# One hybrid diffusion layer on one core: value rows copied whole, transposes and first scores tied in the program order, value stores held back, and one table set for log and exp

## The chip, the core and the metric

The kernel runs on one core of one Trainium2 chip. The core has a matrix engine (TensorE, PE in the profile; its weight loads are PEld), a vector engine (VectorE, DVE), a scalar engine for functions and copies (ScalarE, ACT), a general engine (GpSimd, POOL) and a queue that only issues transfers (SyncE, SP). Each engine runs its own instructions strictly in a fixed order, and waits on semaphores where it needs the work of another. The metric is the time of one execution on the device in microseconds (us), as the median of several runs.

## What is computed

One layer of a diffusion backbone over 1024 latent tokens and 256 context tokens, D = 1024, in float32:

```python
px = modulate(rms_norm(x, norm1_w[i]), sh1, sc1) @ w_in[i]
pc = modulate(rms_norm(ctx, norm1_w[i]), csh1, csc1) @ w_in[i]
...
dn_x, _, _ = gated_deltanet(px[..., :DN_IN], ..., s_ctx_f, s_ctx_b)
...
na_x = neighborhood_attention(qx, kx, vx, kc, vc, na_rpb[i], rows)
x = x + g1 * (jnp.concatenate([dn_x, na_x], axis=-1) @ w_out[i])
x = x + g2 * swiglu(modulate(rms_norm(x, norm2_w[i]), sh2, sc2), w_ffn_in[i], w_ffn_out[i])
```

`gated_deltanet` (group A, 4 heads of 128) runs a short convolution and SiLU over q, k and v, builds a triangular system for each chunk, and scans the chunks forward and backward; its output is gated by SiLU(z). `neighborhood_attention` (group B, 8 heads of 64) normalises q and k, and for each query takes one softmax over a window of the 16 x 64 grid and all context keys. All norms are of the form x * rsqrt(mean(x*x) + eps).

## The kernel before

Each float32 operand of a large product is split into a high and a low half, and each product is made of three matmuls (hi*hi, lo*hi, hi*lo): `hh`, `hl` are the halves of the normed input, `whi`, `wlo` those of weights. Casts to the high half are on ACT (L198, L584), the subtractions for the low half on POOL (L199, L585).

**Stages.** The norm and the modulation come first (to about 40 us), then the input projection as a list of jobs (to about 580), then attention and scan together (to 806), the output projection (to 906) and the feed-forward part (to the end).

**The jobs** stand in the list `jobs`: Blocks k0 to k3 and z1, nk0 to nk2, nv0, nk3, q0 to q3, nq0 to nq3, v0, nv1, v1 to v3 and last z0. A Block is one 128-wide column block of the projection: its matmuls go k-step by k-step (L404; a k-step is one of 8 slices of D, six matmuls of 512 columns or a few more), then `evac` copies PSUM out (for a convolution block on ACT, L452, into `cr`; then VectorE makes the five taps, L456 and L460, into `cacc`), `silu` follows on ACT (L467), `norm` for the attention's q and k (nq, nk) takes Ln and Exp on ACT (L492, L494, L496) and then a scale on VectorE, and `finish` makes transposes and stores. For v heads `finish` transposes `cacc` (L526), scales into `vt` (L530) and stores it to `v_d` from ACT's queue (L534). A Wide job (nv: the attention's values, z: the gate) keeps token tiles stationary and takes 256 columns of weights `zw` in two halves of 128, both of which each of its matmuls (L592) reads. Its `prefetch` loads the halves one after the other through one single buffer `wraw` (L583), casts on ACT (L584) and subtracts on POOL (L585). nv tiles are stored to `nv_d`; after each nv job 64 copies in memory (L1104) lay out that half's values by query column block in `vw_d`, and attention loads windows from it (L277).

**Beside the jobs** run two generators, stepped once for each k-step: `block_inverses` (decay tables; inverts all 32 x 32 diagonal blocks of the chunk systems, with a chain on VectorE over the tile `N`, L880 to L885, and then transposes N on PE, L892) and `preps` (for each chunk and direction the rest of the triangular inverse: decay rows `rg` from POOL, L952; their products on PE, L964; Exp on ACT, L968; a product with the key matrix, L984; copies back on ACT, L987; three substitution steps, L995 to L998). A `yield` in them decides how far apart in the jobs their pieces are written; within that, the build orders the instructions of each engine by its own estimate of when they can run, unless an instruction is kept in program order.

**Queues.** SP issues nearly all transfers in one fixed order, and each waits at its head for what it needs. ACT's function tables are loaded by an instruction of their own (ACT_TABLE_LOAD) wherever the next function is not in the set last loaded; the build places these. One column of buffers (`kx`, 3 of them) is shared by `vt`, the gate tile `zg` and others.

**Attention and scan.** `pair` makes the scores of two heads (L302), the bias and softmax (L304 to L308), transposes (L313, L316) and the product with the values (L323). Its first steps are taken between the tiles of z0 (`next(fill)`); the scan (L1212 and on) is mixed in afterwards, and loads v, k, y and others through L1160.

Of the kernel before, what the change touches and what calls it, by code (L numbers as in the profile page):

```python
# [26 lines left out]
NCH = T // 128  # L27
# [61 lines left out]
def hybrid(ctx, tc, a, dbg):  # L89
# [59 lines left out]
    vw_d = dram.tile([128, 4, 4, 4, 128], F32, name="vw_d", tag="vw_d")  # L149
# [23 lines left out]
    act.activation(sc2, c2, AF.Silu)  # L173
    bg = Background()
# [78 lines left out]
    def attention(nw):  # L253
# [21 lines left out]
        def values(hp, half, cb):  # L275
            vw = nw.tile([128, 3, 128], F32, name="vw", tag="vw", bufs=3)
            sp.dma_start(vw, vw_d[:, hp, cb, half:half + 3])  # L277
            return vw

        def context(hp):  # L280
            vc = nw.tile([128, 2, 128], F32, name="vc", tag="vc")
            sp.dma_start(vc, nv_d[0:CT, hp * 128:hp * 128 + 128].rearrange("(c p) d -> p c d", p=128))
            return vc

        def pair(heads, bts, vw, vc, half, cb, out):
# [4 lines left out]
            for u, (head, w0, bt) in enumerate(zip(heads, WIN, bts)):  # L290
                qs, kh, kl = head
                q = qs[:, (half * 4 + cb) * 128:(half * 4 + cb + 1) * 128]
                kv = [kx[:, CT:].rearrange("p (r c) -> p r c", c=64)[:, r0:r0 + 12, BLKS[cb]:BLKS[cb] + 32]
                      for kx in (kh, kl)]
                parts = [(CTX[w0].start, CTX[w0].stop, (kh[:, 0:CT], kl[:, 0:CT]))]
                if w0:
                    parts += [(256, 512, [x[:, 0:8] for x in kv]), (512, 640, [x[:, 8:12] for x in kv])]
                else:
                    parts += [(0, 384, kv)]
                for n0, n1, ks in parts:  # L300
                    for i in range(2):
                        pe.matmul(sc[:, u * 640 + n0:u * 640 + n1], q, ks[i], start=i == 0, stop=i == 1)  # L302
                m = mx[:, u]
                dve.tensor_tensor_reduce(bt, sc[:, u * 640:u * 640 + 640], bt, -1.0, 3.0e38, OP.add, OP.min,  # L304
                                         m[:, 0:1])
# [68 lines left out]
    with ExitStack() as bs:  # L374
# [32 lines left out]
        class Block:  # L407
# [111 lines left out]
            def finish(self):  # L519
                kind, acc, i = self.kind, self.acc, self.i  # L520
                if kind in "kv":
# [12 lines left out]
                    (act if kind == "v" else sp).dma_start(dst[:, i * 128:(i + 1) * 128].rearrange("(c p) d -> p c d", p=128), vt)  # L534
# [5 lines left out]
                if kind in "kq":  # L540
# [20 lines left out]
                    sp.dma_start(dst[:, :, i], kk[:, c0:])  # L561

        class Wide:
# [32 lines left out]
            def tiles(self):  # L596
# [18 lines left out]
                for t in range(2, NCH):  # L615
# [18 lines left out]
                    act.activation(zt[:, :256], p[:, :256], AF.Silu)  # L634
# [132 lines left out]
        def decay_tables(gp):  # L767
# [4 lines left out]
            act.activation(nA, adt[:, 0:8], AF.Exp)  # L772
# [47 lines left out]
        def block_inverses():  # L820
            with ExitStack() as gs:
# [64 lines left out]
                for _ in range(4):  # L886
                    yield
                U = WK.rearrange("p d u i -> p (d u) i")
                for i0 in range(0, 32, 4):
                    p = bank()  # L890
                    for i in range(4):
                        pe.transpose(p[:, i * P:(i + 1) * P], N[:P, :, :, i0 + i].rearrange("p b r -> p (b r)"),  # L892
                                     ident[:P, :P])
# [16 lines left out]
        done = set()  # L910

        def preps():

            first_half.close()
            with ExitStack() as gs:
# [28 lines left out]
                def prep(i, got):  # L944
# [13 lines left out]
                    if i == 0:  # L958
                        yield 1
                    es = []  # L960
                    for d, c, kk, xc, at in got:
                        p = bank("pr")
                        for j in range(2):
                            pe.matmul(p, mr[:, d], fl(rgs[2 * d + j]), start=j == 0, stop=False)  # L964
# [38 lines left out]
                stores, tick = [], [0]  # L1003
# [45 lines left out]
        for n in range(2, len(jobs) + 2):  # L1049
# [47 lines left out]
            if isinstance(j, Wide) and j.kind == "nv":  # L1097
                hv = slice(2 * j.half, 2 * j.half + 2)
                vlat = nv_d[CT:].rearrange("(r c) d -> r c d", c=64)
                for cb in range(4):  # L1100
                    for ch in range(4):
                        for r in range(4):
                            rows = vlat[4 * ch + r, BLKS[cb]:BLKS[cb] + 32].rearrange("c (h d) -> c h d", d=128)
                            sp.dma_start(vw_d[r * 32:r * 32 + 32, hv, cb, ch], rows[:, hv])  # L1104
            if nrm:
                nrm.norm()
            if isinstance(j, Block):
                j.silu()

# [330 lines left out]
    def normed(t):  # L1440

        s, p = HV[t], bank()
        pe.matmul(p, ones, acc[:, s], start=True, stop=True)  # L1443
        act.activation(rs[:, s], p, AF.Ln, bias=b_eps, scale=1.0 / D)
# [328 lines left out]
```

## Time and profile before

| | |
|---|---|
| Median of 3 runs | 1543.63 us |
| Lowest and highest run | 1539.69 and 1545.23 us |
| The profiled execution | 1541.49 us |
| Its span, first to last instruction | 1539.4 us |
| Mean granted clock of TensorE | 0.988 |
| ACT table loads | 39, of 1.28 us each |

The span is what the profile resolves; the 2.1 us around it are not in it. Rows of a timeline give the start, the duration, the engine, the line, the operation and the tiles; in brackets the idle time of that engine just before and what ended it. `x3` at the end of a row stands for several instructions in one stretch. Rows of a view by stretches give busy time for each engine, the clock that TensorE was granted (1.00 is full, 0.50 half) and the mean busy share of the 16 DMA engines.

### The profile page before, as it was taken

To read this page: it belongs to the slowest core of one execution; us is meant where nothing else is said; L and a number is where in the kernel's file an instruction comes from. 1 tells how busy PE (TensorE), PEld (TensorE's weight loads), DVE (VectorE), ACT (ScalarE), POOL (GpSimd) and SP (SyncE) were. 2 spreads that over 40 slices of the span, in tenths; PEclk is the share of its full clock that TensorE was granted. 3 is DMA by queue.
4 is the path that set the end of the run, shared out by engine and by line. 5 is a ranking of instruction groups with operands and counts; after the bars stand their busy time and mean duration, and the time that the engine had idled before them with its cause. 6 is when DMAs were issued, how large, how long until landed. Compare 5 with 4: busy or idle time off the path is not lost. (4 is left out here: it accounts for less than half of the span.)

```text
span 1539.4 us, 24029 instructions
## 1 busy us (share of the span) xinstructions
PE 1474.1 (96%) x8702; PEld 1231.0 (80%) x8702; DVE 993.6 (65%) x1712; ACT 728.2 (47%) x1405; POOL 234.8 (15%) x286
## 2 busy tenths in 40 slices
PE   6999998899899898999999999999999999999999
PEld 3788797777688787788888878888888888888887
DVE  4774587974464354677977379855555566599652
ACT  5442552646764236666873176333333334354440
POOL 1054500634554100111210000000000000000000
PEclk9999999999999999999999999999999999999999
DMA  9274232687655557898638503533333334798742
GB/s 387 68 212 139 60 86 79 202 239 246 182 172 170 147 142 247 278 292 253 209 90 282 183 34 109 186 106 106 107 105 103 104 102 148 248 376 275 247 143 82
DMA packets 205142, 267.36 MB, mean 174 GB/s; under 512 B 17760, under 2 KB 115552, under 8 KB 204000
## 3 DMA queue, kind: packets, MB, share of 16 engines
q1 hardware_dynamic: 194320, 258.45, 52.4%
q10 hardware_dynamic: 10704, 7.38, 1.5%
q8 instruction: 68, 1.11, 0.3%
q14 instruction: 50, 0.41, 0.1%
HBM read 201.02 MB, written 68.94 MB: 175 GB/s over the span
## 5 line engine op out<-in xcount | busy, mean ns | idle before, releaser
L404 PE MATMUL blk<-hh,whi 128*128 128x512 f32 (+1 forms) x410 | 123.0, 394 | 6.8 <-ACT cr L452 5.3
L1410 ACT CAST uhi<-ws 128x512 fp32r<-128x512 f32 x91 | 54.0, 621 | 146.0 <-PE ps L1349 96.1
L1410 ACT CAST uhi<-wq 128x512 fp32r<-128x512 f32 x101 | 61.0, 622 | 130.9 <-issue 84.6
L404 PE MATMUL blk<-hl,whi 128*128 128x512 f32 (+1 forms) x410 | 115.4, 375 | 0.3 <-DVE hl L704 0.3
L404 PE MATMUL blk<-hh,wlo 128*128 128x512 f32 (+1 forms) x410 | 114.6, 375 | 0.6 <-POOL wlo L199 0.6
L592 PE MATMUL blk<-zw,hh 128*128 128x256 f32 (+1 forms) x576 | 113.5, 291 | 1.1 <-ACT cr L452 1.0
L1411 DVE TENSOR_TENSOR ulo<-wq,uhi 128x512 fp32r<-128x512 f32 x101 | 67.5, 687 | 58.4 <-ACT uhi L1410 32.4
L1349 PE MATMUL ps<-hT,uhi 128*128 128x512 f32 x336 | 103.6, 390 | 0.0
L1349 PE MATMUL ps<-lT,uhi 128*128 128x512 f32 x336 | 103.5, 389 | 0.0
L1349 PE MATMUL ps<-hT,ulo 128*128 128x512 f32 x336 | 103.4, 389 | 0.0
L592 PEld LDWEIGHTS blk<-zw,hh 128*128 128x128 f32 x576 | 91.7, 191 | 4.0 <-ACT cr L452 1.5
L1349 PE MATMUL ps<-hB,uhi 128*128 128x512 f32 x288 | 89.2, 391 | 0.6 <-ACT hB L1524 0.6
L1349 PE MATMUL ps<-lB,uhi 128*128 128x512 f32 x288 | 88.8, 389 | 0.4 <-DVE lB L1525 0.4
L1349 PE MATMUL ps<-hB,ulo 128*128 128x512 f32 x288 | 88.6, 389 | 0.0
L404 PEld LDWEIGHTS blk<-hh,whi 128*128 128x128 f32 x410 | 69.0, 194 | 21.9 <-ACT cr L452 6.1
L404 PEld LDWEIGHTS blk<-hl,whi 128*128 128x128 f32 x410 | 72.5, 192 | 14.9 <-DVE hl L704 0.8
L404 PEld LDWEIGHTS blk<-hh,wlo 128*128 128x128 f32 x410 | 72.5, 192 | 14.9 <-POOL wlo L199 0.9
L592 PE MATMUL blk<-zw,hl 128*128 128x256 f32 (+1 forms) x288 | 82.4, 286 | 0.0
L199 POOL TENSOR_TENSOR wlo<-wraw,whi 128x1024 fp32r<-128x1024 f32 x18 | 46.6, 2586 | 194.1 <-ACT whi L198 193.9
L1349 PEld LDWEIGHTS ps<-lT,uhi 128*128 128x128 f32 x336 | 63.1, 188 | 13.2
L1349 PEld LDWEIGHTS ps<-hT,ulo 128*128 128x128 f32 x336 | 63.1, 188 | 13.2
L1349 PEld LDWEIGHTS ps<-hT,uhi 128*128 128x128 f32 x336 | 62.9, 188 | 12.9
(362 smaller groups left out, 3526.1 us busy)
## 6 DMA issues: line engine op xcount, KB each, us to landing
wq<-w_fo SPq DMA_DIRECT2D x99, 256.0 KB, 4.1
wq<-w_gu SPq DMA_DIRECT2D x88, 256.0 KB, 2.9
wad<-wa SPq DMA_DIRECT2D x64, 256.0 KB, 4.2
bt<-rpb SPq DMA_DIRECT2D x64, 192.0 KB, 3.7
t_d<-g SPq DMA_DIRECT2D x22, 512.0 KB, 3.7
fr<-t_d SPq DMA_DIRECT2D x44, 256.0 KB, 5.2
f_d<-g SPq DMA_DIRECT2D x33, 256.0 KB, 2.1
fr<-f_d SPq DMA_DIRECT2D x33, 256.0 KB, 4.2
```

Source lines behind the costliest of these rows:

```text
L199: lo_engine.tensor_tensor(o, r, h.bitcast(F32), OP.subtract)
L404: pe.matmul(o, ww[:, k], xx[k][:, s], start=k == 0 and j == 0, stop=k == KT - 1 and j == 2)
L592: pe.matmul(p[:, :c1 - c0], x[k][:, s], ww[:, k, c0:c1], start=k == 0 and j == 0, stop=k == KT - 1 and j == 2)
L1349: pe.matmul(o, w[wi][:, k], x[xi][:, k], start=first and k == 0 and j == 0, stop=k == n - 1 and j == 2, skip_group_check=True)
L1410: act.copy(hi, self.raw[key])
L1411: dve.tensor_tensor(lo, self.raw[key], hi.bitcast(F32), OP.subtract)
```

## The change

1. **Values in full rows.** `vw_d` is written once, after nv1, by 16 copies of 32 x 4 x 512 values (L1127) instead of 64 copies of 32 x 2 x 128 after each nv job. The load for a head pair takes its 128 columns out of the longer rows.
2. **Stores of v.** v0's store goes out on SP at once; those of v1 to v3 are put in a list and issued on SP by `release()` (L931) after the attention's step between z0's tiles, in program order.
3. **Ties.** The first of each four transposes of N, the first prep's L964 products (now L989) and the first score matmul keep their place in the program; the waiting yields before the transposes are 6 and not 4, and the first prep waits 10 yields there and not 1 (`LATE`).
4. **Tables.** The set with both log and exp is loaded explicitly in four places: behind the first SiLU, at the first Exp of the decay tables (issued behind z1's last gate tile), ahead of the third prep's Exp, and at the feed-forward's norm. The built program has 21 table loads and not 39.

```diff
-    vw_d = dram.tile([128, 4, 4, 4, 128], F32, name="vw_d", tag="vw_d")
+    vw_d = dram.tile([128, 4, 4, 512], F32, name="vw_d", tag="vw_d")
+    def log_exp():
+        tc.keep_in_program_order(act.preload_act_table_set("natural_log_exp_and_others"))
+    log_exp()
-            sp.dma_start(vw, vw_d[:, hp, cb, half:half + 3])
+            sp.dma_start(vw, vw_d[:, cb, half:half + 3, hp * 128:hp * 128 + 128])
-                        pe.matmul(sc[:, u * 640 + n0:u * 640 + n1], q, ks[i], start=i == 0, stop=i == 1)
+                        s = pe.matmul(sc[:, u * 640 + n0:u * 640 + n1], q, ks[i], start=i == 0, stop=i == 1)
+                        while tied:
+                            tc.keep_in_program_order(tied.pop() and s)
-                    (act if kind == "v" else sp).dma_start(dst[:, i * 128:(i + 1) * 128].rearrange("(c p) d -> p c d", p=128), vt)
+                    held.append((dst[:, i * 128:(i + 1) * 128].rearrange("(c p) d -> p c d", p=128), vt))
+                    if kind == "k" or not i:
+                        sp.dma_start(*held.pop())
-                    act.activation(zt[:, :256], p[:, :256], AF.Silu)
+                    gates.append(act.activation(zt[:, :256], p[:, :256], AF.Silu))
-            act.activation(nA, adt[:, 0:8], AF.Exp)
+            with tc.issue_after(gates[-1].ins):
+                act.preload_act_table_set("natural_log_exp_and_others")
+                act.activation(nA, adt[:, 0:8], AF.Exp)
-                for _ in range(4):
+                for _ in range(6):
                     yield
-                        pe.transpose(p[:, i * P:(i + 1) * P], N[:P, :, :, i0 + i].rearrange("p b r -> p (b r)"),
-                                     ident[:P, :P])
+                        t = pe.transpose(p[:, i * P:(i + 1) * P], N[:P, :, :, i0 + i].rearrange("p b r -> p (b r)"),
+                                         ident[:P, :P])
+                        if not i:
+                            tc.keep_in_program_order(t)
+        def release():
+            while held:
+                tc.keep_in_program_order(sp.dma_start(*held.pop(0)))
-                    if i == 0:
+                    for _ in range(LATE if i == 0 else 0):
                         yield 1
-                            pe.matmul(p, mr[:, d], fl(rgs[2 * d + j]), start=j == 0, stop=False)
+                            m = pe.matmul(p, mr[:, d], fl(rgs[2 * d + j]), start=j == 0, stop=False)
+                            if i == 0:
+                                tc.keep_in_program_order(m)
+                        if i == 2 and not es:
+                            log_exp()
                         act.activation(fl(e), p, AF.Exp)
-                        live.append([prep(*landing.pop(0)), 0])
+                        live.append([prep(*landing.pop(0)), 0 if live or len(todo) < NCH - 1 else -LATE])
                     if final and t > 2:
                         next(fill)
+                        release()
-            if isinstance(j, Wide) and j.kind == "nv":
-                hv = slice(2 * j.half, 2 * j.half + 2)
-                vlat = nv_d[CT:].rearrange("(r c) d -> r c d", c=64)
+            if isinstance(j, Wide) and n == values:
+                vlat = nv_d[CT:].rearrange("(n r c) d -> r c n d", r=4, c=64)
                 for cb in range(4):
-                    for ch in range(4):
-                        for r in range(4):
-                            rows = vlat[4 * ch + r, BLKS[cb]:BLKS[cb] + 32].rearrange("c (h d) -> c h d", d=128)
-                            sp.dma_start(vw_d[r * 32:r * 32 + 32, hv, cb, ch], rows[:, hv])
+                    for r in range(4):
+                        sp.dma_start(vw_d[r * 32:r * 32 + 32, cb], vlat[r, BLKS[cb]:BLKS[cb] + 32])
```

The order of instructions on an engine moves in more places than the diff names, since the build places what is not tied. Three places follow, lines being those of each kernel.

On ACT from v1's copies to z0, before: the casts of z0's two weight halves (zw) stand between the v blocks' copies (cr) and SiLUs (cacc); zg is z0's first output tile.

```order
L452 COPY cr<-blk 128x256
L452 COPY cr<-blk 128x512 x2
L584 CAST zw<-wraw 128x8x128
L467 ACT_TABLE_LOAD
L467 ACTIVATE cacc<-cacc 128x1280
L452 COPY cr<-blk 128x256
L452 COPY cr<-blk 128x512 x2
L467 ACTIVATE cacc<-cacc 128x1280
L584 CAST zw<-wraw 128x8x128
L534 DMA v_d<-vt 128x10x128
L452 COPY cr<-blk 128x256
L452 COPY cr<-blk 128x512 x2
```

And of the change, from v1's SiLU on:

```order
L476 ACT_TABLE_LOAD
L476 ACTIVATE cacc<-cacc 128x1280
L461 COPY cr<-blk 128x256
L461 COPY cr<-blk 128x512 x2
L476 ACTIVATE cacc<-cacc 128x1280
L461 COPY cr<-blk 128x256
L461 COPY cr<-blk 128x512 x2
L476 ACTIVATE cacc<-cacc 128x1280
L597 CAST zw<-wraw 128x8x128 x2
L634 COPY zg<-blk 128x256 x4
```

Both casts have moved behind the SiLU of v3, and v1's store has left ACT. On PE z0's matmuls follow v3's directly in both kernels.

On ACT in an nq block (nq2), before: the block's copies out of PSUM, its Square, Ln and Exp, and then the copies (kk) that a prep's substitution on PE waits for.

```order
L437 ACTIVATE cacc<-blk 128x512 x2
L470 ACTIVATE cr<-cacc 128x1024
L492 ACT_TABLE_LOAD
L492 ACTIVATE cr<-m,bias 128x512 x2
L494 ACT_TABLE_LOAD
L494 ACTIVATE cr<-cr,bias 128x1024
L987 COPY kk<-pr 128x512
```

And of the change, at the same place:

```order
L446 ACTIVATE cacc<-blk 128x512 x2
L479 ACTIVATE cr<-cacc 128x1024
L501 ACTIVATE cr<-m,bias 128x512 x2
L503 ACTIVATE cr<-cr,bias 128x1024
L1012 COPY kk<-pr 128x512
```

The two table loads are gone, and nothing else has moved; the other three nq blocks lose theirs too.

On PE in the q block that runs beside the inversion, before: hh, hl with a number are the eight k-steps, m<-cst,N the first eight transposes of N.

```order
L404 MATMUL blk<-hh_134,whi 128x512 x2
L404 MATMUL blk<-hl_135,whi 128x512 x2
L404 MATMUL blk<-hh_134,wlo 128x512 x2
L892 MATMUL m<-cst,N 128x80 x8
L404 MATMUL blk<-hh_451,whi 128x512 x2
L404 MATMUL blk<-hl_452,whi 128x512 x2
L404 MATMUL blk<-hh_451,wlo 128x512 x2
L892 MATMUL m<-cst,N 128x80 x8
```

And of the change:

```order
L413 MATMUL blk<-hh_135,wlo 128x512 x2
L413 MATMUL blk<-hh_452,whi 128x512 x2
L413 MATMUL blk<-hl_453,whi 128x512 x2
L413 MATMUL blk<-hh_452,wlo 128x512 x2
L413 MATMUL blk<-hh_454,whi 128x512 x2
L413 MATMUL blk<-hl_455,whi 128x512 x2
L413 MATMUL blk<-hh_454,wlo 128x512 x2
L907 MATMUL m<-cst,N 128x80 x8
```

Two k-steps (12 matmuls) now stand ahead of the first transposes. VectorE's chain over N is the same in both.

More of the change, by code (lines that the diff above doesn't have):

```diff
@@ L283, in context @@
             return vc
+        tied = [True]
         def pair(heads, bts, vw, vc, half, cb, out):
@@ L561, in finish @@
                     sp.dma_start(dst[:, :, i], kk[:, c0:])
+        gates = []
         class Wide:
@@ L908, in hybrid @@
         fl = lambda x: x.rearrange("p a b -> p (a b)")
-        done = set()
+        done, held = set(), []
+        def release():
+            while held:
+                tc.keep_in_program_order(sp.dma_start(*held.pop(0)))
         def preps():
@@ L1001, in prep @@
                         stores.append((y_d[d, c], y[d], tick[0] + 1))
-                stores, tick = [], [0]
+                LATE, stores, tick = 10, [], [0]
                 def flush(n):
@@ L1108, in hybrid @@
                 j.silu()
+        release()
         dve.tensor_scalar(SQ, SQ, EPS, None, op0=OP.add)
@@ L1443, in normed @@
         pe.matmul(p, ones, acc[:, s], start=True, stop=True)
+        if not t:
+            log_exp()
         act.activation(rs[:, s], p, AF.Ln, bias=b_eps, scale=1.0 / D)
```

## The prediction

> **What bounds the kernel now.** I read the page first, then the stretches, then the list of what TensorE (PE) waits for. In the page, one line settles which engine sets the time:
>
> ```profile
> PE 1474.1 (96%) x8702; PEld 1231.0 (80%) x8702; DVE 993.6 (65%) x1712; ACT 728.2 (47%) x1405; POOL 234.8 (15%) x286
> ```
>
> PE is busy for 1474 of 1539 us, so this change, which removes no PE work, can only move waits of PE and the clock. The busy time of each stretch (columns: length, then PE, PEld, DVE, ACT, POOL, granted PE clock, DMA share, GB/s) shows where waits are:
>
> ```profile
> 250.00:304.00 54.00, 44.11 (x205) 34.61 (x204) 43.29 (x39) 25.02 (x38) 22.97 (x19) 0.87 0.51 163
> 366.00:447.00 81.00, 73.68 (x480) 57.30 (x479) 42.65 (x47) 59.50 (x104) 46.32 (x48) 0.96 0.63 192
> 525.00:556.00 31.00, 24.65 (x128) 20.70 (x128) 14.02 (x22) 8.39 (x11) 5.82 (x6) 0.89 0.95 253
> 585.00:640.00 55.00, 44.92 (x409) 37.67 (x409) 31.10 (x87) 37.29 (x92) 5.34 (x14) 1.00 0.86 279
> 906.00:1539.40 633.40, 628.96 (x2778) 520.03 (x2778) 416.18 (x661) 254.03 (x438) 0.00 (x0) 1.00 0.46 155
> ```
>
> The last row is the feed-forward part: 4.4 us idle in 633, nothing to win. The other four are the places the change touches. By whom PE waits there (total us, times, longest):
>
> ```profile
> PE pr L995 <- ACT kk L987: 7.3, 6, 2.1
> PE m L892 <- DVE N L885: 5.7, 1, 5.7
> PE blk L404 <- ACT cr L452: 5.3, 1, 5.3
> PE sc L302 <- DVE mx L304: 3.3, 4, 1.6
> PE pr L964 <- POOL rg L952: 2.7, 4, 0.9
> PE pr L984 <- DVE kk L971: 1.1, 1, 1.1
> PE blk L592 <- ACT cr L452: 1.0, 1, 1.0
> PE ps L1349 <- ACT hB L1524: 0.6, 1, 0.6
> ```
>
> A wait costs more than its length, because the clock falls behind it. Of PE alone (length, busy, granted clock, DMA share, GB/s):
>
> ```profile
> 255.84:262.66 6.82, 4.17 (x16) 0.50 0.19 50
> 293.38:300.21 6.83, 5.83 (x17) 0.50 1.01 315
> 399.20:402.60 3.40, 3.40 (x9) 0.50 0.49 111
> 443.57:446.98 3.41, 3.41 (x21) 0.50 0.77 223
> 532.30:539.10 6.80, 4.59 (x13) 0.50 1.08 255
> ```
>
> Work under a clock of 0.50 takes twice as long, so half of each row's busy time is lost: 2.1, 2.9, 1.7, 1.7 and 2.3 us.
>
> **The change, part by part.** The sum is made against the profiled execution, 1541.49 us; the median of the three runs, 1543.63, lies 2.1 above it.
>
> *One log and exp table, in the nq blocks.* In the second nq block ScalarE (ACT) runs:
>
> ```profile
> 390.75 1.28 ACT L492 ACT_TABLE_LOAD   x1
> 394.27 1.28 ACT L494 ACT_TABLE_LOAD   x1
> 396.62 1.05 ACT L987 COPY kk<-pr 128x512 f32<-128x512 f32 x2
> 397.24 0.25 PE L995 MATMUL pr<-y,kk 128*32 128x32 f32 x2 [2.01 <-ACT kk L987]
> ```
>
> Both loads stand ahead of the copy that PE waits for; in the changed order they are gone from all four nq blocks and the copy moves 2.56 us forward. No single L995 wait is longer than 2.1, so all 7.3 us go, and with them both short half-clock rows (1.7 each): 10.7. I take **10.5**, for a remainder of 0.2; bounds 5 (the clock still falls and something else holds the copy) and 10.7.
>
> The wait of 2.01 us that ends at 397.24 is followed by 3.4 us at clock 0.50. [...]
>
> *Six yields in the block inverses.* The first transposes of N now stand two k-steps later on PE, while VectorE's chain is as it was:
>
> ```profile
> 249.62 0.62 PE L404 MATMUL blk<-hh,whi 128*128 128x512 f32 x2
> 250.98 0.61 PE L404 MATMUL blk<-hh,whi 128*128 128x512 f32 x2
> 257.95 0.17 DVE L885 MEMSET N<- 80x128 f32 x1
> 258.17 0.53 PE L892 MATMUL m<-cst,N 80*128 80x80 f32 x2 [5.66 <-DVE N L885]
> ```
>
> A k-step is 1.36 us (250.98 less 249.62), so 2.7 of the wait is covered; 2.9 stay, and behind a wait of that length the clock still falls (the 2.01 above), for one short row, 1.7 instead of 2.1. **3.1**; bounds 2.5 (clock row as now) and 4.8 (clock kept).
>
> *LATE = 10 and the ties in the first prep.* L964's four waits (2.7), L984's (1.1) and the half-clock row (2.9) are 6.7 at most. But in the changed order the first prep's L1009 matmuls and then four L1020 matmuls follow one another on PE without a projection matmul between: L1020 waits there for the copy of L1009's result. [...] The tied matmuls also hold the projection behind them if xc's fx copies, queued behind the stores of x_d, come late, up to some 3.5 us. **3.0**; bounds -1 (a gap of 3.5, the 1.2, and the clock still low) and 6.7.
>
> *Start and feed-forward.* The two loads of norm1 go, but behind them L702's wait is for VectorE, fed by the modulation's weights; the pair at the feed-forward's start can return at most L1349's 0.6. **0.4**, bounds 0 and 1. In the nk blocks no wait of PE for ACT stands in the list, so their loads are hidden now.
>
> *Values in full rows, z0's weights.* This is the costly part. Before, and on the clock of that trace:
>
> ```profile
> 525.45 0.61 SPq L583 DMA_DIRECT2D wraw<-w_z  x1
> 530.57 1.05 ACT L584 CAST zw<-wraw 128x1024 fp32r<-128x1024 f32 x1 [13.89 <-DMA wraw<-w_z]
> 531.70 2.35 POOL L585 TENSOR_TENSOR zw<-wraw,zw 128x1024 fp32r<-128x1024 f32 x1 [2.47 <-ACT zw L584]
> 534.51 0.80 PE L404 MATMUL blk<-hh,whi 128*128 128x512 f32 x1 [5.32 <-ACT cr L452]
> 543.58 1.03 ACT L584 CAST zw<-wraw 128x1024 fp32r<-128x1024 f32 x1
> 544.69 2.40 POOL L585 TENSOR_TENSOR zw<-wraw,zw 128x1024 fp32r<-128x1024 f32 x1 [10.64 <-ACT zw L584]
> 551.54 1.35 ACT L452 COPY cr<-blk 128x256 f32<-128x256 f32 x3 [6.93 <-PE blk L404]
> 552.94 0.38 PE L592 MATMUL blk<-zw,hh 128*128 128x256 f32 x1 [1.03 <-ACT cr L452]
> 559.86 1.28 ACT L467 ACTIVATE cacc<-cacc 128x1280 f32<-128x1280 f32 x1 [0.55 <-DVE cacc L460]
> ```
>
> ACT's cast of w_z's first half waited for a load that SP issued only at 525.45, behind the small vw_d stores; v2's copies were queued behind the cast, and PE stood 5.32 us. In the changed order both casts stand behind the silu of v3. That frees v2's copies: of 5.32 I leave 1.0 (the wait that the L592 row shows at the next boundary), which with the clock's 2.3 gives **+6.6**; bounds 5 and 7.6 (nothing left of the 5.32).
>
> But z0 follows v3 directly on PE, and its matmuls read both halves of zw. From v3's copies at 551.54: silu starts at 559.86 behind the convolution and ends at 561.14; first cast 1.05; first subtraction on POOL 2.35, to 564.5; only then is the single buffer free for SP's second load, 5.1 us as from 525.45 to the cast at 530.57, to 569.6; second cast 1.03; second subtraction 2.40, to 573.1. PE can do half a microsecond of z0 ahead of that. So z0 starts some 19.5 us later than at 552.94, nothing else stands on PE in that time, and behind so long a pause I charge 2.5 of half clock (between 1.7 and 3.4, one or two short rows). **-22**; bounds -19 (a load of 3.9 us instead, no more than one clock row) and -25. SP's loads for the next heads wait behind the second half too, but are wanted only by scores that stand behind z0.
>
> *Stores of v kept back, first scores tied.* v's stores leave ACT's queue (four issues) and go behind the heads' loads; their consumer is the scan. On PE the scan begins one score group earlier, beside softmax waits such as L302's 3.3. **1.0**; bounds -3 and +4.
>
> Sum: 10.5 + 3.1 + 3.0 + 0.4 + 6.6 - 22 + 1.0 = 2.6 us gained: 1538.9 on the profiled execution, 1541.0 on the median. I forecast **1540**, between the two. All good ends together give 10.7 + 4.8 + 6.7 + 1 + 7.6 - 19 + 4 = 15.8, all bad ones 5 + 2.5 - 1 + 0 + 5 - 25 - 3 = -16.5.
>
> **The rivals.**
>
> 1. *The gaps close better than I allow*: N's wait and the first prep leave no half clock (4.8 and 6.7), the attention returns 3, and z0's second half lands in 3.9 us (-20.5). 10.7 + 4.8 + 6.7 + 0.4 + 6.6 - 20.5 + 3 = 11.7: **1531**. For it: each is an edge the rows allow. Against it: the first prep's new tie. Chance 0.25.
>
> 2. *z0 isn't starved*, the change keeping its gains at no price: 2.6 + 22 = 24.6, **1518**. It needs the casts to be free of v3's silu, which the fixed order excludes, or v3's convolution to be early, for which no row speaks. Chance 0.06.
>
> 3. *Slower: the sixteen vw_d copies hold w_z back.* They move 4.2 MB in one go between about 497 and w_z, and SP can issue w_z's first load only behind them.
>
> ```profile
> 490.92 30.98 SPq L1104 DMA_DIRECT2D vw_d<-nv_d  x46
> 497.00:521.00 24.00, 23.94 (x166) 19.61 (x165) 8.08 (x12) 5.14 (x10) 2.40 (x1) 1.00 0.19 51
> vw_d<-nv_d SPq DMA_DIRECT2D x128, 32.0 KB, 2.2
> ```
>
> Before, 46 of them took SP 31 us; in 24 of these, with hardly anything else in the queue, the DMA engines moved 51 GB/s and were 0.19 busy; from that share an estimate of 51 / 0.19 = 270 GB/s makes 16 us of the whole, and w_z is there by 521. It decides if w_z lands after 561.1, when ACT is free: 4.2 MB in 59 us, below 71 GB/s. At the 51 GB/s of the row the copies would end at 579, w_z land at 584, and z0 start 23 later still: **1563**; half way, 1552. Against it: the low share. Chance 0.16.
>
> 4. *The clock does not fall behind waits of 2 us*, and the two short rows come from something else that stays: the nq term is 7.1 and the total **1543**. The first of them stands right behind such a wait, which speaks against it. Chance 0.03. [...]
>
> **How the numbers follow.** My forecast has 0.50, with its own range of 1533 to 1548. 0.5% of 1543.6 is 7.7 us, about what a measurement here can tell from no change: faster is below 1535.9, slower above 1551.3. Faster: 0.06 + most of rival 1 (0.20) + 0.09 of the forecast's low end = 0.35. Slower: 0.14 of rival 3 and 0.04 of the forecast's bad end = 0.18. Within: 0.47. The range 1522 to 1556 leaves out rival 2 and half of rival 3, with a little of each end.
>
> **What would show it.** Right: no table load between the nq blocks' L501 and L503, no L1020 wait on ACT above 0.5 and full clock from 366 to 447; one PE wait of 18 to 21 us ahead of z0's first L605 matmul, ending with POOL's L598; both zw casts behind v3's silu. Wrong: an L605 wait below 10 us (rival 2); w_z's first load landing after v3's silu (rival 3); a wait above 4 us at L1009 or L1020, which would sink the prep term; L907 with no wait, which would raise the fourth.

## The result and the profile after

| | median, us | lowest to highest | runs |
|---|---|---|---|
| Changed kernel | 1537.48 | 1533.48 to 1538.84 | 13 |
| Kernel before, beside it | 1540.61 | 1537.73 to 1545.70 | 13 |

The ratio, taken from runs beside one another, is 0.9973, 95% interval 0.9962 to 0.9985: some 4 us faster (the two medians lie 3.1 apart), inside the half per cent that was called no change. The profiled execution took 1538.76 us, its span is 1537.0 against 1539.4. From the page of the changed kernel, the line of busy times:

```profile
PE 1469.1 (96%) x8702; PEld 1230.5 (80%) x8702; DVE 992.6 (65%) x1712; ACT 705.2 (46%) x1387; POOL 234.6 (15%) x286
```

PE is as full as before and has the same 8702 matmuls; its busy time is 5 us less, in part since less of it ran at half clock (31.5 us before, 26.8 now, the start included). That the span fell by only 2.4 is the sum of large pieces. The list of PE's waits (total, times, longest):

```profile
PE blk L605 <- ACT zw L597: 18.2, 1, 18.2
...
PE ps L1236 <- DMA y<-y_d: 4.4, 2, 3.8
PE m L494 <- ACT cr L479: 3.1, 1, 3.1
...
PE pr L1020 <- ACT kk L1012: 2.0, 3, 1.2
PE pr L1020 <- DVE y L1022: 1.9, 1, 1.9
PE m L907 <- DVE N L900: 1.7, 1, 1.7
...
PE blk L605 <- POOL zw L598: 1.2, 1, 1.2
PE pr L1009 <- DVE kk L996: 1.2, 1, 1.2
```

The waits of before (7.3 for kk, 5.7 for N, 5.3 for cr, 2.7 for rg) are gone or small. In their place stands one wait of 18.2 us. The stretches of PE at half clock beyond the start (length, busy, granted clock, DMA share, GB/s):

```profile
297.30:300.70 3.40, 3.40 (x10) 0.50 0.95 289
437.24:440.66 3.42, 3.42 (x13) 0.50 0.12 28
532.82:556.70 23.88, 6.65 (x29) 0.50 0.53 143
597.67:601.08 3.41, 3.23 (x13) 0.50 0.94 326
```

Of six before, five stand in the prediction (the sixth, 3.4 us at 170.5, lies ahead of all that the change touches). Now the long one begins in z0's wait of 18.15 us and holds 6.65 us of work, of which half, 3.3, is counted as lost. The prediction, too, counts work at clock 0.50 as twice as long; in the traces it is a little less: pairs of L404 matmuls start 0.85 us apart at 0.50 (from 399.92 before the change) and 0.46 at 1.00 (from 403.75), and three of z0's matmuls take 0.64 (from 553.15 in the change) and 0.36 (from 558.03).

The matmuls of the two traces are in the same stages, so the same matmul can be looked up in both, and the difference of its start times says what each stage gave in these two profiles (before minus after):

| stage | forecast | measured |
|---|---|---|
| start, up to 233 us | part of 0.4 | 0.3 |
| N's inverse and the first prep, 233 to 348 | 3.1 + 3.0 | 6.7 |
| nq blocks, 348 to 499 | 10.5 | 6.7 |
| v2 to v3, 523 to 540 | 6.6 | 7.5 |
| z0's weights, 551 to 583 | -22 | -21.4 |
| attention and scan, 583 to 897 | 1.0 | 1.3 |
| feed-forward's start, 897 to 922 | part of 0.4 | 1.3 |
| sum | 2.6 | 2.4 |

The timeline of the changed kernel around z0 (start, duration, engine; idle time before and what ended it in brackets):

```profile
504.17 0.61 SPq L596 DMA_DIRECT2D wraw<-w_z  x1
...
530.32 1.35 ACT L461 COPY cr<-blk 128x256 f32<-128x256 f32 x3 [5.77 <-PE blk L413]
538.69 1.27 ACT L476 ACTIVATE cacc<-cacc 128x1280 f32<-128x1280 f32 x1 [7.02 <-DVE cacc L469]
539.86 1.03 ACT L597 CAST zw<-wraw 128x1024 fp32r<-128x1024 f32 x1
540.97 2.34 POOL L598 TENSOR_TENSOR zw<-wraw,zw 128x1024 fp32r<-128x1024 f32 x1 [35.82 <-ACT zw L597]
543.34 0.60 SPq L596 DMA_DIRECT2D wraw<-w_z  x1
547.75 1.04 ACT L597 CAST zw<-wraw 128x1024 fp32r<-128x1024 f32 x1 [6.86 <-DMA wraw<-w_z]
548.85 0.58 PE L605 MATMUL blk<-zw,hh 128*128 128x256 f32 x1 [18.15 <-ACT zw L597]
...
551.27 0.79 PE L605 MATMUL blk<-zw,hh 128*128 128x256 f32 x2 [1.21 <-POOL zw L598]
```

The first half of w_z is asked for at 504.17, 35 us ahead of its cast, and landed 4.0 us later. ACT was idle for 7.02 us between v3's copies and v3's silu, with the weights there and the cast standing behind the silu. The cast has no idle time in brackets: it waited for its turn only. Then the single buffer makes the second half go the whole way again.

### The profile page after: what moved, and what is told of

Its sections match the earlier page's. It is cut to its first block, busy times and chain, and to the rows that moved or that the text cites. A ratio compares the mean times of both kernels' runs of the same rounds, so it can differ in the third digit from the quotient of the medians.

```text
span 1537.0 us, 23902 instructions
## 1 busy us (share of the span) xinstructions
PE 1469.1 (96%) x8702; PEld 1230.5 (80%) x8702; DVE 992.6 (65%) x1712; ACT 705.2 (46%) x1387; POOL 234.6 (15%) x286
## 4 chain that ended last, share of the span: by engine, by line
PE 51%; ACT 0%; DVE 0%; issue 0%; ACTq 0%
PE ps L1373 28%; PE ps L1716 14%; PE ps L1502 3%; PE ps L1350 1%; PE ps L1524 1%; PE sc L332 1%; PE sc L322 1%; PE sc L309 1%; PE ps L1248 0%; PE ps L1236 0%; PE ps L1253 0%; PE ps L1227 0%; PE ps L1217 0%; PE ps L223 0%; PE ps L1155 0%; ACT pt L325 0%
## 5 line engine op out<-in xcount | busy, mean ns | idle before, releaser
L605 PE MATMUL blk<-zw,hh 128*128 128x256 f32 (+1 forms) x576 | 115.8, 295 | 20.5 <-ACT zw L597 18.2
```

What stands on the lines that cost most here:

```text
L605: pe.matmul(p[:, :c1 - c0], x[k][:, s], ww[:, k, c0:c1], start=k == 0 and j == 0, stop=k == KT - 1 and j == 2)
```

## The experiments

A theory and its rivals. **Theory:** the change's parts gain some 24 us, and the place of z0's two casts takes nearly all of it back; what is left of the nq blocks' waits is held by other instructions. **Rivals:** the large vw_d copies hold w_z back whatever the order of the casts; the tables' gain comes only with the rest; z0's hole is filled by scores at no loss, so that the tie is what costs. Every kernel was timed beside the kernel before on the same chip, and its ratio is to that.

**1. z0's casts ahead of v3's.** In the changed kernel v3's copies are issued behind the first cast and its silu behind the second. Otherwise it is the same work, and PE's order is the same.

```diff
...
-                j.evac()
+                with tc.issue_after(jobs[-1].casts[0]) if n == len(jobs) - 2 else ExitStack():
+                    j.evac()
...
-                j.silu()
+                with tc.issue_after(jobs[-1].casts[1]) if n == len(jobs) - 2 else ExitStack():
+                    j.silu()
```

> The change, with one edge in ScalarE's order: v3's copies out of PSUM stand behind the cast of z0's first weight half, v3's SiLU behind the second. Theory A (z0 starves because its casts stand behind v3's SiLU on ScalarE): first cast at about 524.6 us (v2's SiLU ends there), subtraction to 528, second load 5 us to 533, cast, subtraction to about 536.5, so TensorE waits some 5 us ahead of z0 instead of 19.4, half clock behind it 1.7 instead of 3.3: about 1537.5 - 16 = 1521.5 us, a ratio to before near 0.988. Theory B (the transfers are late: the sixteen value copies and SP's queue hold z0's weights): the wait stays above 15 us and the time within 1533 to 1540.

Measured: 1522.89 us, ratio 0.988 (0.9863 to 0.9897). PE's waits for zw in this kernel:

```profile
PE blk L606 <- ACT zw L598: 2.9, 1, 2.9
...
PE blk L606 <- POOL zw L599: 2.1, 1, 2.1
```

Of 19.4 us 5.0 remain, and the time falls by 14.6, a little less than the 16 expected. So most of what the forecast charged came from the order of two casts on ACT, and not from a load that arrived late.

**2. z0's casts one block earlier still.** The prefetch is made in two steps: the first half during v2, with v2's copies behind the first cast, the second during v3 with v3's copies behind the second, which is kept in program order.

```diff
-            if n + 1 < len(jobs):
+            if n + 1 < len(jobs) - 1:
...
+            if n in (len(jobs) - 3, len(jobs) - 2):
+                jobs[-1].prefetch((n - len(jobs) + 3,))
...
-                j.evac()
+                i = n - len(jobs) + 3
+                with tc.issue_after(jobs[-1].casts[i]) if i in (0, 1) else ExitStack():
+                    j.evac()
```

> The change, with z0's first weight half traced one job earlier: its cast stands ahead of v2's copies, the second cast ahead of v3's copies. Theory A: first cast at about 514 us, second load landed by 523, second subtraction done near 528, before v3 ends at 530.7, so the wait ahead of z0 falls to about 1 us and the half clock behind it goes: 1537.5 - 18.4 - 3.3 = about 1516 us, ratio near 0.984. If attention and scan have a bound of their own (loads or softmax), part of the 21.7 us comes back after z0 as waits there and the time is 1520 to 1530. Theory B: no better than e1, 1533 to 1540.

Measured: 1516.9 us, ratio 0.9835 (0.982 to 0.985), 20.6 under the change. No wait for zw is left; z0's first matmul waits 0.94 us for v3's copies. In the kernel before the same early cast stopped v2's copies for 5.32 us, because w_z came late behind the small stores. Now it does not:

```profile
514.27 1.28 ACT L476 ACTIVATE cacc<-cacc 128x1280 f32<-128x1280 f32 x1 [8.56 <-DVE cacc L469]
515.45 1.03 ACT L599 CAST zw<-wraw 128x1024 fp32r<-128x1024 f32 x1
```

The cast follows the silu of v1 with no wait, and v2's copies come at 516.38. This is about the time of the forecast's second rival (1518, z0 not starved), which the change as it stands could not reach.

**3. The tables alone.** The kernel before with only part 4 of the change.

```diff
...
+    log_exp()
...
-            act.activation(nA, adt[:, 0:8], AF.Exp)
+            with tc.issue_after(gates[-1].ins):
+                act.preload_act_table_set("natural_log_exp_and_others")
+                act.activation(nA, adt[:, 0:8], AF.Exp)
...
+                        if i == 2 and not es:
+                            log_exp()
...
+        if not t:
+            log_exp()
```

> The kernel before, with nothing but the table set for log and exp (21 loads and not 39). Theory A: the gain in the nq blocks (6.7 us in the change's trace) and at the feed-forward's start (1.3) is the tables' alone: 7 to 9 us below before, ratio 0.994 to 0.9955; L995's waits fall from 7.3 to 2 to 4 us, the wait of 5.3 us between v2 and v3 stays. Rival: the nq gain needs the changed order of the rest, and this alone gives under 3 us.

Measured: 1531.81 us, ratio 0.9938 (0.9924 to 0.9951). This excludes the rival by which the tables gain only with the rest. Between the matmuls of 348 and 499 us 8.1 us are gained, and 1.3 at the feed-forward's start. (This profile also lost 4.5 us between 583 and 897, where it had two stretches at half clock, at 587.6 and 611.5.) Its waits of PE:

```profile
PE blk L409 <- ACT cr L457: 5.1, 1, 5.1
PE m L901 <- DVE N L894: 4.5, 1, 4.5
...
PE pr L1006 <- DVE y L1008: 1.9, 1, 1.9
```

L995's waits for kk (7.3 before; the line is L1006 here) fall to 0.4. The wait of 1.9 us for VectorE's copy y appears with the tables alone. N's wait is 4.5 instead of 5.7, though nothing of the inverse was touched.

**4. The value rows alone.** The kernel before with only part 1.

```diff
-    vw_d = dram.tile([128, 4, 4, 4, 128], F32, name="vw_d", tag="vw_d")
+    vw_d = dram.tile([128, 4, 4, 512], F32, name="vw_d", tag="vw_d")
...
-            if isinstance(j, Wide) and j.kind == "nv":
+            if isinstance(j, Wide) and n == values:
...
+                    for r in range(4):
+                        sp.dma_start(vw_d[r * 32:r * 32 + 32, cb], vlat[r, BLKS[cb]:BLKS[cb] + 32])
```

> The kernel before, with nothing but the values in full rows. Theory C (this part alone moves the build's order, since the build takes z0's weights to be late): both casts stand behind v3's SiLU, and first scores ahead of z0; the 5.3 us between v2 and v3 and their half clock go (-6.6), z0 waits 20 us or more with half clock behind it: slower than before by 12 to 20 us, ratio 1.008 to 1.013. Rival: the casts were moved by another part, and this one alone is 5 to 8 us faster than before.

Measured: 1552.95 us, ratio 1.0073 (1.006 to 1.0087): slower, by a little less than the 12 to 20 us expected. It gains 7.5 us from v2 to v3, exactly what the whole change gains there, and loses 18.9 between 551 and 583. So both belong to this part: the build, which orders by its own estimate what isn't tied, now puts both casts behind v3's silu, ties or not. (That its estimate takes w_z to be late is the likely reason; the estimate itself was not looked at.) But PE's hole is another one here. SP's longest wait between 530 and 560 us, and then the timeline:

```profile
SPq L583 <- DMA v_d<-vt: 32.6, 1, 32.6
```

```profile
540.18 0.38 ACTq L534 DMA_DIRECT2D v_d<-vt  x1
543.90 0.62 SPq L583 DMA_DIRECT2D wraw<-w_z  x1
...
551.28 0.58 PE L302 MATMUL sc<-kh,qs 128*128 128x256 f16 x2 [8.07 <-DMA kh<-nk_d]
```

SP held w_z's load until the store of v1 from ACT's queue had landed, and the heads' loads stood behind it, so the scores that were built ahead of z0 waited 8.07 us for kh. That wait for the store is in the built program: the two transfers are given the same completion counter (semaphore 102 in the trace). The prediction saw nothing of it. In the change the stores are kept back and w_z is issued at 504.17, and the tie puts the scores behind z0; what each of these is worth, experiments 6 and 7 tell.

**5. The inverse and the first prep alone.** The kernel before with the six yields, the ties there, and LATE = 10.

```diff
-                for _ in range(4):
+                for _ in range(6):
                     yield
...
+                        if not i:
+                            tc.keep_in_program_order(t)
...
-                    if i == 0:
+                    for _ in range(LATE if i == 0 else 0):
                         yield 1
...
```

> The kernel before, with nothing but the later, tied transposes of N and the later, tied first prep. Theory A: what the change's trace shows up to 348 us (7 us ahead of before) is this part's alone: L892's wait falls from 5.7 to under 2, L964's and L984's from 3.8 to about 1.2, and one new wait of some 3 us comes for the squares of a q block (VectorE's conv taps are mixed with the transposes): 5 to 7 us faster, ratio 0.9955 to 0.997. Rival: the gain up to there belongs to the table set or the value rows, and this part alone gives under 2 us.

Measured: 1537.21 us, ratio 0.9976 (0.9964 to 0.9988), some 3.7 us and short of the 5 to 7 expected. In the trace the stage from 233 to 348 us gives 1.5. Its waits of PE:

```profile
PE m L485 <- ACT cr L470: 3.1, 1, 3.1
PE m L892 <- DVE N L885: 2.7, 1, 2.7
```

N's wait falls from 5.7 to 2.7, near the 2.9 of the forecast. The rest of the way to 1.7 in the changed kernel is that of experiments 3 and 4, in which the chain on VectorE ends about 1 us earlier (waits of 4.5 and 4.8). The wait of 3.1 us at L485 is new, and belongs to this part.

**6. The stores of v back on ACT's queue.** The changed kernel, with part 2's stores undone and the score's tie kept.

```diff
-                    held.append((dst[:, i * 128:(i + 1) * 128].rearrange("(c p) d -> p c d", p=128), vt))
-                    if kind == "k" or not i:
-                        sp.dma_start(*held.pop())
+                    (act if kind == "v" else sp).dma_start(dst[:, i * 128:(i + 1) * 128].rearrange("(c p) d -> p c d", p=128), vt)
```

> The change, with all four stores of v put back on ScalarE's queue. Theory A (z0 starves by ScalarE's order alone): z0's first load now shares a completion slot with v1's store and is issued only behind it, near 532 us, still ahead of its cast at 539.9; z0's wait stays 18 to 20 us, and the scan's wait for y (3.8 us at 594) shrinks below 2: 1535 to 1539. Rival (the stores held back are what keeps z0's weights from being later still): the cast itself waits for the load and the time rises to 1543 or more.

Measured: 1541.03 us, ratio 0.9991 (0.9973 to 1.0009), above the 1535 to 1539 expected and below its rival's 1543. The scan's wait for y falls from 3.8 to 1.7, as expected if v's loads on SP hold it up, but no time comes of it. SP stands ahead of w_z again:

```profile
SPq L594 <- DMA v_d<-vt: 32.5, 1, 32.5
```

Here that costs nothing, and z0's wait stays (17.8 and 1.2): the cast comes behind v3's silu anyway, and the tied scores want kh only behind z0. An early cast as in experiment 2 would be another matter, which wasn't tried with the stores on ACT. Against the change's 0.9973 the intervals overlap: whether the stores' new place gains a little is open, that it loses is not borne out.

**7. The first scores free.** The changed kernel without the tie of the first score matmul to the gate tile.

```diff
-        tied = [True]
+        tied = []
```

> The change, without the tie of the first score matmul: in the built order both first score groups and two transposes stand ahead of z0 on TensorE, and an Exp between z0's two casts on ScalarE. Theory A: z0 still starts near 550 us since its second cast is no earlier, but some 3 us of scores are done in the hole and the softmax waits at 585 to 590 shrink: 1531 to 1536. Rival: the Exp ahead of the second cast and the transposes ahead of z0 push z0 back by what the scores save or more: 1537 to 1545.

Measured: 1531.78 us, ratio 0.9938 (0.9918 to 0.9959), 5.7 under the change. In the hole ahead of z0 now stand scores, with waits of their own:

```profile
537.92 0.37 PE L309 MATMUL sc<-kh,qs 128*128 128x256 f16 x1 [6.41 <-DVE mx L313]
...
542.59 0.66 PE L322 MATMUL sc<-cst,bt 128*128 128x128 f32 x2 [3.44 <-DVE bt L317]
...
546.87 0.58 PE L605 MATMUL blk<-zw,hh 128*128 128x256 f32 x1 [3.62 <-ACT zw L597]
```

The tie therefore costs 5.7 us while z0 is starved; what it costs with the casts moved early was not tried. It is a price of the hole and not its cause: with scores in it these three waits still make 13.5 us.

**8. LATE at 16**, on experiment 2.

```diff
-                LATE, stores, tick = 10, [], [0]
+                LATE, stores, tick = 16, [], [0]
```

> The second kernel with casts moved (e2_casts_before_v2, 1516.9), with the first prep 16 yields late and not 10. If the waits of the first prep (L1009 1.2 us, decay rows) are what is left there, they go: 1 to 2 us below e2. If the wait for the squares of a q block (3.1 us, and 6.8 us at half clock around it) is VectorE's backlog and not the prep's place, it stays 2 to 3 us and the time within 1514 to 1518; and if preps now run into the v blocks, waits appear there and it is slower than e2.

Measured: 1512.7 us, ratio 0.9813 (0.9795 to 0.9831) against 0.9835 (0.982 to 0.985). The wait for kk near 369 us (1.32 in experiment 2) and the 3.4 us at half clock behind it are gone. From 233 us on the traces are 2.5 us apart; the timed intervals just overlap. The first prep's own wait for VectorE's product (L1009 in the changed kernel), which was expected to go, is still there with 1.4 us.

**9, 10, 11. What was left of the two new waits.** On experiment 8: the sums of squares in the q blocks a step later (9), the fifth prep's copy y on ACT (10), both (11).

```diff
-                    p = bank()
-                    for c in range(8):
-                        pe.matmul(p[:, c:c + 1], r[:, t0 + c * 128:t0 + (c + 1) * 128], M[C_ONE][:, 0:1],
-                                  start=True, stop=True)
-                    dve.tensor_copy(SQ[:, :, i], p[:, 0:8])
...
+                    p = bank()
+                    for c in range(8):
+                        pe.matmul(p[:, c:c + 1], self.r[:, self.t0 + c * 128:self.t0 + (c + 1) * 128],
+                                  M[C_ONE][:, 0:1], start=True, stop=True)
+                    dve.tensor_copy(SQ[:, :, i], p[:, 0:8])
+                    yield
```

```diff
-                        dve.tensor_copy(y[0][blk[0], :, cols[0]], ps[0][blk[0], :, :32 * n])
+                        (act.copy if i == 5 else dve.tensor_copy)(y[0][blk[0], :, cols[0]], ps[0][blk[0], :, :32 * n])
```

> The version with z0's weights cast early and LATE at 16, with one more edit: in the q blocks the eight matmuls of the squares' sums and VectorE's copy of them are traced in the step finish, a step later than norm. Theory A: TensorE's wait of 3.1 us at L494 is for VectorE's (and ScalarE's) backlog at one moment and nothing else stands on that chain, so the wait and the half clock behind it go: 3 to 6 us less than without the edit (1512.7), 1507 to 1510, ratio 0.977 to 0.980. Theory B: the next thing on the same chain (the copy of the sums, then rg, which the products of finish need) is late in its turn, and less than 1 us comes: 1512 to 1515.

> The version with z0's weights cast early and LATE at 16, with one more edit: the fifth prep's copies into y[0] (the ones that TensorE waits 1.9 us for near 433) run on ScalarE instead of VectorE. Theory A: the copy was late only because VectorE had v0's convolution ahead of it, so the wait goes, and with it a half-clock row where there is one: 2 to 3.5 us less than without the edit (1512.7), 1509 to 1511. Theory B: ScalarE has its own queue there (kk copies, casts of weights) and the copy or those behind it come late instead: 1512 to 1516, with a wait for ScalarE at L1020 or its like.

> Both edits together, on the version with z0's weights cast early and LATE at 16. If both waits are separate, as theory A of each says, their gains add: 1504 to 1508, ratio to the kernel before 0.976 to 0.978. If both are late for a common reason (VectorE's whole backlog through the projection), the second edit adds under 1 us to the better of the two.

| | median, us | ratio | interval |
|---|---|---|---|
| 9, squares later | 1508.85 | 0.980 | 0.9778 to 0.9822 |
| 10, y on ACT | 1512.57 | 0.9825 | 0.9801 to 0.985 |
| 11, both | 1510.78 | 0.9806 | 0.9782 to 0.983 |

Busy time of PE from 280 to 345 us (length, busy, clock, DMA share, GB/s), first in experiment 8, then in 9:

```profile
280.00:345.00 65.00, 60.46 (x370) 0.95 0.76 237
```

```profile
280.00:345.00 65.00, 64.85 (x420) 1.00 0.83 262
```

Fifty matmuls more are done in the same 65 us: the 3.1 us wait is gone, and nothing follows it. In the traces this is 6.5 us, of which 3.4 are two half-clock rows that experiment 8's profile had. The medians are 3.9 apart, but the ratios only 0.9813 and 0.980, with intervals that overlap. In experiment 10 the wait of 1.9 us is gone, but its neighbours are new:

```profile
432.93 0.61 PE L1025 MATMUL pr<-y,kk 128*32 128x64 f32 x14 [0.76 <-ACT y L1028]
...
435.28 0.71 PE L990 MATMUL pr<-rg,mr 128*128 128x512 f32 x2 [0.96 <-ACT y L1027]
```

0.76 and 0.96 us, now for ACT, in the place of 1.9 for VectorE: no gain, as its second theory had it, and none on top of 9. Experiment 9 has the lowest median of the study, 2% under the kernel before (interval 1.8 to 2.2%) and by the two ratios 1.7% under the change; from 8 and 11 the intervals do not tell it apart.

## Why the prediction was right, and where it was not

The forecast was 1540, the change measured 1537.5 beside a kernel before that itself ran at 1540.6. Ratios are the fairer test: the forecast's 1540 is 0.9976 of 1543.63 and its sum, 1541.0, is 0.9983; measured 0.9973. That the sum came out is in part luck: the nq term fell 3.8 us short, and the other stages were better than forecast by 0.6, 0.9, 0.6, 0.3 and 1.2. Of the forecast's own signs, the one on nq failed (an L1020 wait for ACT of 1.18 us, and half clock at 437); those on z0 held. By its steps:

- **z0's weights (-22; -21.4).** Shown. The wait is 18.15 + 1.21 = 19.4 where 19.5 was forecast, ends with POOL's L598, and both casts stand behind v3's silu. The second load took 4.4 us (543.34 to 547.75) instead of 5.1; the half clock took 3.3 instead of 2.5. Experiment 1 gives 14.6 us of it back by moving the two casts on ACT alone, experiment 2 20.6 by moving them and their loads.
- **v2's copies freed (+6.6; +7.5).** Shown by experiment 4 to be the value rows' doing. Of the 5.32 nothing stayed, the forecast's upper edge.
- **The tables in the nq blocks (+10.5; +6.7): the step that was mis-sized.** The mechanism held: the loads are gone, and so are most waits for kk. What failed is "all 7.3 us go, and with them both short half-clock rows". What is late next had to be looked for, as the prediction itself asked. Of the changed kernel, in two places:

```profile
365.78 1.05 ACT L203 CAST whi<-wraw 128x1024 fp32r<-128x1024 f32 x1 [1.71 <-DMA wraw<-w_nqk]
...
366.73 1.15 ACT L503 ACTIVATE cr<-cr,bias 128x1024 f32<-128x1024 f32 x1
367.78 1.05 ACT L1012 COPY kk<-pr 128x512 f32<-128x512 f32 x2
368.49 0.22 PE L1020 MATMUL pr<-y,kk 128*32 128x32 f32 x2 [1.18 <-ACT kk L1012]
...
435.33 0.29 DVE L1022 COPY y<-pr 32x128 f32<-32x128 f32 x1
435.77 0.64 PE L1020 MATMUL pr<-y,kk 128*32 128x64 f32 x16 [1.92 <-DVE y L1022]
```

```profile
347.60:499.40 151.80, 143.93 (x1056) 0.98 0.63 192
```

```profile
340.60:485.70 145.10, 140.81 (x1049) 0.99 0.67 206
```

  The first copy kk stands behind a weight cast that waited 1.71 us for its transfer. The other wait is for a copy on VectorE, queued behind v0's convolution and nq's halves; behind it the clock fell (the row at 437.24), which costs 1.7 more. The last two rows are PE's busy time in the stretch, before and after: in place of 7.9 us of idle PE there are 4.3 (151.8 less 143.93, and 145.1 less 140.81). Experiments 1, 2, 6 and 7, whose matmuls stand in the same order up to there, gain 6.0 to 7.3 in this stretch, so the shortfall is not one profile's. With the tables alone (experiment 3) it is 8.1 gained, since the kk wait near 367 is not there: it comes with the first prep's new place and goes with LATE at 16.
- **N and the first prep (3.1 + 3.0; 6.7 together): the sum is right by luck.** N's wait fell by 4.0 us, from 5.7 to 1.7, and in this profile the clock stayed full behind it, which saves the 2.1 of before as well: 6.1 where 3.1 was forecast. It is 1.7 and not 2.9 because two other parts bring VectorE's chain forward. That leaves some 0.6 for the first prep in place of 3.0. Its waits for rg are gone, and its feared ties cost nothing visible. No run shows the 1.2 that the lower bound counts at L1020: a copy kk took 0.59 (L987 before, L1012 now), L1020 has no wait in the list up to 340 us, and L1009 keeps 1.2. But a wait of 3.1 us stands at L494, which the prediction did not have. How far the clock at N was luck, experiments 1, 2, 6 and 7 tell: with the matmuls in the same order and N's wait at 1.7 to 1.8 us the clock fell behind it in all four, and the stage gave 4.1 to 5.5 us. Experiment 5 gives these edits only some 3.7 of the total time by themselves. The new wait, in the changed kernel:

```profile
290.77 1.48 DVE L920 TENSOR_TENSOR WK<-WK,NB 128x1280 f32<-128x1280 f32 x1
292.18 1.27 DVE L469 SCALAR_TENSOR_TENSOR cacc<-cr,cw,cacc 128x1022 f32<-128x1022 f32 x1
...
294.57 1.06 ACT L479 ACTIVATE cr<-cacc 128x1024 f32<-128x1024 f32 x1
295.68 2.13 PE L494 MATMUL m<-ones,cr 128*128 128x1 f32 x16 [3.13 <-ACT cr L479]
```

  The q block's convolution on VectorE is mixed with the inverse's last steps (L917, L920), so silu and square come late on ACT and the sums of squares on PE with them. The matmuls that had been there to cover it, the first prep's, were moved away.
- **The feed-forward's start (0.4 in all; 1.3).** The forecast counted only L1349's 0.6 wait. VectorE's lB, the next wait there, hung on the same chain, and one whole table load (1.28 us) was on the path; experiment 3 has the same 1.3.
- **Stores and first scores (+1.0; +1.3).** The net is right, its parts are not: the tie costs 5.7 (experiment 7) inside the z0 stage, and the stores' new place spares SP a stand of 32.5 us, which was seen to cost only where scores are ahead of z0 (experiment 4, not 6).

Of the rivals, the third (vw_d copies hold w_z back) is excluded by the load issued at 504.17, which had landed long before its cast; part 1 alone was slower all the same, by the place of the casts. The store of v1 is the smaller part of that: with the scores free and the stores kept back (experiment 7) the profile loses 16.6 us from 540 to 583, in experiment 4 18.9. The first did not come: N and the first prep gave 6.7 of its 11.5, the nq term 6.7 of its 10.7. The fourth is refuted by the trace of the change itself: a wait of 1.92 us at 433.8 was followed by 3.4 us at half clock.

## What to carry to other kernels

A cast or copy that waits for nothing but its turn is seen by the missing bracket in its row: look there at the engine's idle time just ahead (7.02 us here) and move the instruction into it, before anything else is tuned. When a stall is taken away, list what the waiting instruction needs next, on every engine, and charge the second-latest of them; here that was a third of the largest gain forecast. And make a data layout change together with the order that its estimate sets, because the build may answer it by moving work that the edit never names, as in experiment 4.

## What the runs showed of the hardware

**The granted clock and PE's idle time.** In all thirteen traces the granted clock changes only on a grid of 3.41 us whose start differs from run to run; before the change the stretches beyond the start are 3.41 or 6.83 us at half clock and 30.72 to 136.53 at full between them, all multiples of 3.41. I added up PE's idle time in each slot at full clock, past the first 40 us. Every one of the 40 slots with more than 1.81 us of it was followed by a slot at half clock. Of 77 with 1.29 to 1.81 us 23 were, and with less, 2 of some 5400 (in the traces of before and after alone: 6 of 6, 4 of 17, none of 833). Those two, in experiments 8 and 10, had no idle time at all, and no run shows why the clock fell there. The same wait was followed by full clock in one run and by half in another. N's wait of 1.75 us, which starts at 254.9 in both, first in the changed kernel, then in experiment 1:

```profile
252.92:256.34 3.42, 2.02 (x9) 1.00 0.07 20
256.34:259.75 3.41, 2.66 (x15) 1.00 0.00 0
```

```profile
255.57:258.98 3.41, 1.89 (x11) 1.00 0.00 0
258.99:262.39 3.40, 3.40 (x15) 0.50 0.00 0
```

With 1.40 us idle in its slot the clock stayed at 1.00; with 1.52 the next slot was at 0.50.

**Profiles of the same code differ at the start.** At the same matmul near 233 us, ahead of which most of these kernels are alike, the traces of before, after and experiments 1 to 8 lie up to 4.0 us apart; the stages above are therefore compared from there on. A half-clock slot of 3.41 us more or less, counted as half lost, is 1.7 us in a single profile, so a difference smaller than that is read from medians of several runs.

**A transfer waited for one of another queue.** In experiments 4 and 6 SP stood 32.6 and 32.5 us ahead of a load until a store issued by ACT had landed, with no data in common; in both the load and the store carry the same semaphore, 102.
